# Other places for loads and roundings in a hybrid encoder block: attention's ends, the passage to the mixer, odd blocks' buffers

## The chip, the cores and the metric

The kernel runs on one core of one Trainium2 chip. The metric is the device time of one execution in microseconds (us), as the median of three runs. The engines are TensorE (PE, matmuls; PEld is its weight load), VectorE (DVE), ScalarE (ACT), GpSimd (POOL) and SyncE (SP), which here issues every DMA.

## The reference

One layer of an encoder block on 1024 tokens of width 1024 with 16 learned meta tokens in front, in float32:

```
xn = rmsnorm(h)
q, k, v, xr, gr, gates = split(xn @ w_in)
attn = softmax(rope(norm(q)) rope(norm(k))^T / sqrt(128)) v     # 8 query heads, 2 kv heads of 128, no mask
rnn  = (forward RG-LRU + backward RG-LRU)(conv(xr)) * gelu(gr)
h    = h + (sigmoid(g_attn) * attn + sigmoid(g_rnn) * rnn) @ w_out
h    = h + (silu(n @ w_gate) * (n @ w_up)) @ w_ffn_out          # n = rmsnorm(h), inner width 2816
```

## The kernel before

**Split operands.** A float32 operand is split into a rounded part (hi) and the remainder (lo), and a product of two such operands is three matmuls (hi hi, hi lo, lo hi). `split` (L95 to L97) does it: ACT writes hi (L96), then DVE, or POOL where the caller asks for it, writes lo as source minus hi (L97). So each operand that TensorE reads has a load by SP into a raw buffer, a rounding on ACT and a remainder on DVE or POOL. The pool of raw buffers has three; fifteen larger buffers are called pages.

**Attention** works in tiles (h, i): head h, 128 queries i of 8, all 1040 keys. `emit_scores` multiplies nine matmuls into one of two sets of score banks (S), DVE takes the maximum (L668), ACT the exponential and its sum (L671), which frees the banks, DVE scales the sum and takes its reciprocal (L673, L674). ACT then writes two copies in 16 bit (L677 and the small L678), DVE the residuals (L680, two per tile), and SP issues a transposing DMA. A weighted sum over values (`emit_pv`, 25 matmuls into a bank pv) follows for each pair of tiles, some tiles later; DVE multiplies it with the gate (L696), POOL adds the recurrent part (L697), and the result goes out to memory as the mix.

Between the tiles TensorE gets steps of six matmuls. In heads 0 to 5 they are the gate projection of the next head (`ga_steps`, bank gap, L719 to L721), whose result ACT takes out as a sigmoid (L626). In heads 6 and 7 rests of the gate steps come first and then pieces of the output projection (`out_steps`, bank oph, L763 to L765), which need M (the stored mix, loaded again and split) and wo (blocks of w_out); DVE adds their result to the residual h (L768). The table `ahead` says at which tile each M, wo and x is loaded and split. The gate of head 0 (ga, both halves of the tokens) is projected as a whole before attention begins.

**Passage to the mixer.** The last output tiles (t = 4 to 7) alternate with the second norm. For each token tile DVE makes sums of the transposed rows, which enter the mixer's products as T1 to T4 and B. For t = 4 to 7 POOL adds the hi and lo parts of the lower tokens first (`wholes`), and `norm2_upper` uses the sums.

**Mixer.** The first FFN matrix is done in 22 blocks of 128 columns by a scheme with seven products instead of eight (A11B11, A12B21, S3T3, S2T2, S1T1, A22T4, S4B22), each twelve matmuls. The S operands are sums of quarters of the weight block (`prep`, L966 to L980), made from two raw loads. A11 and A12 of the first three blocks are prepared early (`prep_early`). POOL sums the results of pairs of blocks and the rows of w_ffn_out for the second matrix (`act_sums`, `wout_sums` L1065 to L1068) after every block or pair.

**Order.** The program is written tile by tile. A planner then sets a fixed row of instructions for each engine, by its own estimate of when inputs are there; a row need not follow the program's text, and each engine works its row in order.

## Time and profile before

| | us |
|---|---|
| median of three runs | 1514.45 |
| lowest, highest | 1508.05, 1516.13 |
| the profiled execution | 1514.26 |
| its span | 1512.5 |
| busy: PE, DVE, ACT, POOL | 1477.2, 1090.7, 743.9, 256.9 |

The profiled execution is one run; its span lies between its first and last instruction, and 1.8 us of its time lie outside. Busy time is the time in which an engine executes at least one instruction. The granted clock of PE, 0.993 in the mean, is told as a share of full speed.

### The profile page before, as it was taken

To read this page: it belongs to the slowest core of one execution; us is meant where nothing else is said; L and a number is where in the kernel's file an instruction comes from. 1 tells how busy PE (TensorE), PEld (TensorE's weight loads), DVE (VectorE), ACT (ScalarE), POOL (GpSimd) and SP (SyncE) were. 2 spreads that over 40 slices of the span, in tenths; PEclk is the share of its full clock that TensorE was granted. 3 is DMA by queue.
4 is the path that set the end of the run, shared out by engine and by line. 5 is a ranking of instruction groups with operands and counts; after the bars stand their busy time and mean duration, and the time that the engine had idled before them with its cause. 6 is when DMAs were issued, how large, how long until landed. Compare 5 with 4: busy or idle time off the path is not lost. (4 is left out here: it accounts for less than half of the span.)

```text
span 1512.5 us, 20066 instructions
## 1 busy us (share of the span) xinstructions
PE 1477.2 (98%) x7323; PEld 1240.3 (82%) x7323; DVE 1090.7 (72%) x1695; ACT 743.9 (49%) x1242; POOL 256.9 (17%) x195
## 2 busy tenths in 40 slices
PE   7999999999999899999999999999999999999998
PEld 5888888888888788888778877888888888888887
DVE  6877676666666878777755697888888877557562
ACT  5544477766676676767642452333333332454330
POOL 0000000000000533324320203433333333200000
PEclk9999999999999999999999999999999999999999
DMA  7123311222211789889995216555444444798641
GB/s 245 57 70 98 91 31 61 63 63 63 63 56 57 168 192 198 197 194 235 201 198 174 83 44 194 169 166 165 159 162 155 160 160 153 272 369 286 214 146 58
DMA packets 302275, 222.62 MB, mean 147 GB/s; under 512 B 150776, under 2 KB 244432, under 8 KB 302176
## 3 DMA queue, kind: packets, MB, share of 16 engines
q1 hardware_dynamic: 302176, 221.34, 50.0%
q8 instruction: 57, 0.93, 0.3%
q14 instruction: 42, 0.34, 0.1%
HBM read 133.21 MB, written 52.43 MB: 123 GB/s over the span
## 5 line engine op out<-in xcount | busy, mean ns | idle before, releaser
L96 ACT ACTIVATE pw<-pr 128x1024 fp32r<-128x1024 f32 x77 | 81.1, 1061 | 106.5 <-PE po L1181 63.5
L96 ACT ACTIVATE wS<-s 128x512 fp32r<-128x512 f32 x88 | 53.2, 628 | 151.6 <-DVE s L966 56.8
L1179 PE MATMUL po<-pw 128*128 128x512 f32 x308 | 119.8, 389 | 0.0
L1180 PE MATMUL po<-pw 128*128 128x512 f32 x308 | 119.8, 389 | 0.0
L1181 PE MATMUL po<-pw 128*128 128x512 f32 x308 | 119.8, 389 | 0.0
L97 DVE TENSOR_TENSOR pw<-pr,pw 128x1024 fp32r<-128x1024 f32 x77 | 91.6, 1222 | 37.4 <-ACT pw L96 31.9
L680 DVE SCALAR_TENSOR_TENSOR PP<-p,pr,PP 128x1024 f16<-128x1024 f32 (+1 forms) x128 | 103.1, 864 | 11.8 <-ACT PP L677 11.6
L671 ACT ACTIVATE p<-S,nm 128x1044 f32<-128x1044 f32 x64 | 72.2, 1128 | 52.9 <-DVE nm L668 50.0
L694 PE MATMUL pv<-PT,vt 128*128 128x256 f16 x800 | 94.7, 276 | 2.0 <-DMA PT<-PP 2.0
L97 DVE TENSOR_TENSOR wA<-raw,wA 128x512 fp32r<-128x512 f32 x66 | 72.7, 1125 | 23.6 <-ACT wA L96 23.6
L694 PEld LDWEIGHTS <-vt 128*128 128x128 f16 x800 | 76.5, 99 | 15.6 <-DMA PT<-PP 2.2
L668 DVE TENSOR_REDUCE nm<-S 128x1 f32<-128x1044 f32 x64 | 78.3, 1237 | 6.5 <-PE S L104 6.0
L677 ACT ACTIVATE PP<-p,pr 128x1040 f16<-128x1040 f32 x64 | 73.9, 1154 | 0.0
L102 PE MATMUL S<-kT,qh 128*128 128x348 f32 (+1 forms) x192 | 63.4, 330 | 7.1 <-ACT p L671 7.1
L1181 PEld LDWEIGHTS po<-pw 128*128 128x128 f32 x308 | 57.8, 188 | 12.1
L1179 PEld LDWEIGHTS po<-pw 128*128 128x128 f32 x308 | 57.8, 188 | 12.1
L1180 PEld LDWEIGHTS po<-pw 128*128 128x128 f32 x308 | 57.8, 188 | 11.8
L103 PE MATMUL S<-kT,qh 128*128 128x348 f32 (+1 forms) x192 | 62.7, 327 | 0.0
L104 PE MATMUL S<-kT,qh 128*128 128x348 f32 (+1 forms) x192 | 62.5, 325 | 0.0
L103 PE MATMUL xr<-xn,wblk 128*128 128x264 f32 (+1 forms) x192 | 61.4, 320 | 0.0
L104 PE MATMUL xr<-xn,wblk 128*128 128x264 f32 (+1 forms) x192 | 61.4, 320 | 0.0
L102 PE MATMUL xr<-xn,wblk 128*128 128x264 f32 (+1 forms) x192 | 61.4, 320 | 0.0
(305 smaller groups left out, 4330.4 us busy)
## 6 DMA issues: line engine op xcount, KB each, us to landing
raw<-in_w_ffn_in_dram SPq DMA_DIRECT2D x47, 512.0 KB, 4.7
raw<-in_w_in_dram SPq DMA_DIRECT2D x44, 512.0 KB, 4.1
pr<-act_d SPq DMA_DIRECT2D x77, 256.0 KB, 5.1
...
```

What stands on the lines that cost most here:

```text
L96: S.activation(out=hi, in_=src, func=AF.Copy)
L97: (eng or V).tensor_tensor(out=lo, in0=src, in1=f32(hi), op=ALU.subtract)
L102: PE.matmul(out=ps, lhsT=lh, rhs=rh, start=(k == 0), stop=False)
L103: PE.matmul(out=ps, lhsT=lh, rhs=rl, start=False, stop=False)
L104: PE.matmul(out=ps, lhsT=ll, rhs=rh, start=False, stop=(k == n - 1))
L668: V.tensor_reduce(out=nm, in_=s[:, :, 0:KC], axis=AX.XY, op=ALU.max, negate=True)
L677: S.activation(out=pair[:, 0:NK], in_=pf, func=AF.Copy, scale=r)
L680: V.scalar_tensor_tensor(out=pair[:, o:o + e - a], in0=pf[:, a:e], scalar=r, in1=pair[:, a:e], op0=ALU.mult, op1=ALU.subtract)
L694: PE.matmul(out=ps, lhsT=vt[:, j, hl, vs], rhs=pt[:, m], start=(n == 0), stop=(n == len(terms) - 1))
L1179: PE.matmul(out=banks[t], lhsT=lh, rhs=w[:, 0, 1], start=j == 0, stop=False)
L1180: PE.matmul(out=banks[t], lhsT=lh, rhs=w[:, 1, 1], start=False, stop=False)
L1181: PE.matmul(out=banks[t], lhsT=ll, rhs=w[:, 0, 1], start=False, stop=j == NFP - 1)
```

## The change

- The gate of head 0 is projected for the first half of the tokens only before attention; the second half becomes four steps ahead of the others, and head 0's first five tiles get 3, 3, 2, 2, 2 steps (before 2, 2, 2, 1, 1). A bank is requested once more at the start of its pool, so that the later banks fall on other places.
- In heads 0 to 5 the loads of the next queries and gate weights are separated from their splits, which stand one or two tiles later.
- In heads 6 and 7 every M and wo has its load at one entry of the table and its split at a later one. The remainders are DVE's instead of POOL's, and ACT's rounding stands behind the copies of a tile (`issue_after`). The residual x of the first four token tiles is no longer loaded into h: the first output half is copied there, and x is loaded into a raw buffer and added later by DVE.
- S3, S2 and their splits of block 0 come at t = 4, together with A11 and A12. POOL's sums for t = 7 are gone; DVE subtracts the two parts one by one.
- Blocks with odd number load into a page (wraw) instead of raw buffers. S4's sum is written over S2's. `wout_sums` runs after blocks 4, 5, 6, 8, 9, 10, 12, 14, 16, 18 and 20.

How the rows move: ACT in head 7, around the exponentials (L671 before, L684 after) of tiles (7,4) and (7,5); the copies are PP, and wo is the rounding of a w_out block. Before:

```order
L677 ACTIVATE PP_4463<-p,pr 128x1040
L678 ACTIVATE PP_4463<-p,pr 128x16
L96 ACTIVATE wo<-raw 128x2x512 x2
L671 ACTIVATE p,den<-S_4460,nm 128x1044
L671 ACTIVATE p,den<-S_4461,nm 128x1044
L677 ACTIVATE PP_4464<-p,pr 128x1040
L678 ACTIVATE PP_4464<-p,pr 128x16
L677 ACTIVATE PP_4465<-p,pr 128x1040
L678 ACTIVATE PP_4465<-p,pr 128x16
```

After, from the copies of the pair before:

```order
L690 ACTIVATE PP_4437<-p,pr 128x1040
L691 ACTIVATE PP_4437<-p,pr 128x16
L684 ACTIVATE p,den<-S_4434,nm 128x1044
L684 ACTIVATE p,den<-S_4435,nm 128x1044
L690 ACTIVATE PP_4438<-p,pr 128x1040
L691 ACTIVATE PP_4438<-p,pr 128x16
L98 ACTIVATE wo<-raw 128x2x512
L690 ACTIVATE PP_4439<-p,pr 128x1040
L691 ACTIVATE PP_4439<-p,pr 128x16
L98 ACTIVATE wo<-raw 128x2x512
L684 ACTIVATE p,den<-S_4434,nm 128x1044
L684 ACTIVATE p,den<-S_4435,nm 128x1044
```

Two roundings stood ahead of the exponentials. Now a pair has one between the copies of its two tiles and one behind them, and the next pair's exponentials follow.

DVE in the passage, after the remainder of T3 of t = 7 (T and B are operands of the products, s sums of weights, c and whole sums of rows, act A12B an addition that waits for the product A12B of block 2). Before:

```order
L97 TENSOR_TENSOR T_8034<-c_8220,T_8033 128x4x128
L911 TENSOR_TENSOR c_8218<-c_8218,whole 128x512
L995 TENSOR_TENSOR act<-act,A12B_8246 128x512
L914 TENSOR_TENSOR whole<-whole,c_8218 128x512
L97 TENSOR_TENSOR T_8040<-c_8218,T_8039 128x4x128
L966 TENSOR_TENSOR s_8265<-raw 128x512
L970 TENSOR_TENSOR s_8270<-raw 128x512
L97 TENSOR_TENSOR T_8282<-whole,T_8281 128x4x128
L97 TENSOR_TENSOR wS_8267<-s_8265,wS_8267 128x512
L972 TENSOR_TENSOR s_8272<-s_8270,raw 128x512
L97 TENSOR_TENSOR T_8278<-whole,T_8277 128x4x128
L97 TENSOR_TENSOR T_8282<-whole,T_8281 128x4x128
```

After:

```order
L99 TENSOR_TENSOR T_8058<-c_8245,T_8057 128x4x128
L955 TENSOR_TENSOR c_8250<-hT,B_7782 128x512
L1051 TENSOR_TENSOR act<-act,A12B_8274 128x512
L956 TENSOR_TENSOR c_8250<-c_8250,B_7783 128x512
L99 TENSOR_TENSOR T_8231<-whole,T_8230 128x4x128
L957 TENSOR_TENSOR c_8244<-c_8244,c_8250 128x512
L99 TENSOR_TENSOR T_8226<-whole,T_8225 128x4x128
L963 TENSOR_TENSOR whole<-whole,c_8183 128x512
L99 TENSOR_TENSOR T_8064<-c_8244,T_8063 128x4x128
L99 TENSOR_TENSOR T_8226<-c_8250,T_8225 128x4x128
L99 TENSOR_TENSOR T_8231<-whole,T_8230 128x4x128
L965 TENSOR_TENSOR c_8251<-B_7786,c_8244 128x512
```

S3's sum (L966) and its remainder (wS) are no longer here. T2's remainder, fifth row before, is the ninth row now (T_8064), behind the two subtractions that stand in for POOL's sum (L955, L956) and work on other tiles.

SP from the store of residual rows h on, to the loads of the mixer's weights. Before:

```order
L947 DMA raw<-in_w_ffn_in_dram 128x8x128
L864 DMA h_d_7549<-h 128x1024
L864 DMA h_d_7550<-h 128x1024
L947 DMA raw<-in_w_ffn_in_dram 128x8x128 x2
L1061 DMA raw<-in_w_ffn_out_dram 128x1024 x2
L1044 DMA act_d_7727<-act 128x512
L947 DMA raw<-in_w_ffn_in_dram 128x8x128
L1044 DMA wot_d_7738<-bs 128x512
L947 DMA raw<-in_w_ffn_in_dram 128x8x128
```

After:

```order
L903 DMA h_d_7542<-h 128x1024
L903 DMA h_d_7543<-h 128x1024
L1001 DMA raw<-in_w_ffn_in_dram 128x8x128 x2
L903 DMA h_d_7544<-h 128x1024
L903 DMA h_d_7545<-h 128x1024
L1001 DMA raw<-in_w_ffn_in_dram 128x8x128 x2
L903 DMA h_d_7546<-h 128x1024
L1001 DMA raw<-in_w_ffn_in_dram 128x8x128
L903 DMA h_d_7547<-h 128x1024
L1001 DMA wraw<-in_w_ffn_in_dram 128x8x128 x2
L1001 DMA raw<-in_w_ffn_in_dram 128x8x128
L1001 DMA wraw<-in_w_ffn_in_dram 128x8x128 x2
```

The two loads of w_ffn_out (L1061) stood between the two loads of block 2; now the loads of block 2 stand ahead of the store of h's last rows, and odd blocks have their own loads (wraw).

The diff:

```diff
@@ line 92 @@
         return ap.bitcast(F32)
-    def split(src, hi, lo, eng=None):
-        S.activation(out=hi, in_=src, func=AF.Copy)
+    def split(src, hi, lo, eng=None, behind=None):
+        with tc.issue_after(behind.ins) if behind else nullcontext():
+            S.activation(out=hi, in_=src, func=AF.Copy)
         (eng or V).tensor_tensor(out=lo, in0=src, in1=f32(hi), op=ALU.subtract)
@@ line 177 @@
         return ps0.tile([128, 512], F32, tag=tag, bufs=bufs, name=name)
-    def load_block(col, eng=None):
+    bank0("gate")
+    def load_block(col, eng=None, later=None):
         raw = raw_tile([128, 8, 128])
...
         w = page([128, 2, 8, 128], F32R, "wblk")
-        split(raw, w[:, 0], w[:, 1], eng)
+        if later is None:
+            split(raw, w[:, 0], w[:, 1], eng)
+        else:
+            later.append(lambda: split(raw, w[:, 0], w[:, 1], eng))
         return w
@@ line 629 @@
     w_ga = next_block()
-    for ps, o, n in project("ga", w, REAL):
+    for ps, o, n in project("ga", w, REAL[:1]):
         gate(ga0[:, 0, o:o + n], ps)
@@ line 650 @@
     n_tile = [0]
+    copies = [None]
     PT = {}
@@ line 675 @@
         S.activation(out=pair[:, 0:NK], in_=pf, func=AF.Copy, scale=r)
-        S.activation(out=pair[:, T + 64:T + 64 + NM], in_=pf[:, T:NK], func=AF.Copy, scale=r)
+        copies[0] = S.activation(out=pair[:, T + 64:T + 64 + NM], in_=pf[:, T:NK], func=AF.Copy, scale=r)
         for a, e, o in ((0, T, KLO), (T, NK, T + 32)):
@@ line 708 @@
         return g
-    def ga_steps(w, gar):
-        for c in range(2):
+    def ga_steps(w, gar, chunks=range(2)):
+        for c in chunks:
             ps = fill_bank("gap")
@@ line 725 @@
     M = [[[None, None], [None, None]], [[None, None], [None, None]]]
-    def load_mix(kh, c, eng=None):
-        for hl in range(2):
-            M[hl][kh][c] = page([128, 4, 512], F32R, f"M{hl}{kh}{c}")
-        for k in range(0, 4, 2):
-            n = 1 if kh and not c and k else 2
-            raw = raw_tile([128, 2, 512])[:, 0:n]
-            SP.dma_start(out=raw, in_=mix_d[kh][k:k + n, :, 512 * c:512 * c + 512].rearrange("h d t -> d h t"))
-            split(raw, M[0][kh][c][:, k:k + n], M[1][kh][c][:, k:k + n], eng)
+    def load_mix(kh, c, k, behind=False):
+        if k == 0:
+            for hl in range(2):
+                M[hl][kh][c] = page([128, 4, 512], F32R, f"M{hl}{kh}{c}")
+        n = 1 if kh and not c and k else 2
+        raw = raw_tile([128, 2, 512])[:, 0:n]
+        SP.dma_start(out=raw, in_=mix_d[kh][k:k + n, :, 512 * c:512 * c + 512].rearrange("h d t -> d h t"))
+        yield
+        split(raw, M[0][kh][c][:, k:k + n], M[1][kh][c][:, k:k + n], behind=copies[0] if behind else None)
+        yield
     wo = {}
...
         wo[j, n] = page([128, 2, 2, 512], F32R, "wo")
-        split(raw, wo[j, n][:, :, 0], wo[j, n][:, :, 1], G)
+        yield
+        split(raw, wo[j, n][:, :, 0], wo[j, n][:, :, 1], behind=copies[0])
+        yield
     hres = {}
-    def load_h(c, alloc, js=range(2)):
-        for j in js:
...
@@ line 765 @@
                 hs = hres[t][:, 512 * n:512 * n + 512]
-                V.tensor_tensor(out=hs, in0=hs, in1=ps, op=ALU.add)
+                if kh == 0 and t < 4:
+                    V.tensor_copy(out=hs, in_=ps)
+                else:
+                    V.tensor_tensor(out=hs, in0=hs, in1=ps, op=ALU.add)
             yield
     def out_steps():
+        for j in range(2):
+            p = page([128, 2, D], F32, "h")
+            hres[2 * j], hres[2 * j + 1] = p[:, 0], p[:, 1]
         for n in range(2):
...
     gar = {0: ga0, 1: load_gar(1)}
-    steps = ga_steps(w_ga, gar[1])
+    steps = chain(ga_steps(w, ga0, [1]), ga_steps(w_ga, gar[1]))
+    items = [
+        ("M00a", load_mix, 0, 0, 0, True), ("M00b", load_mix, 0, 0, 2, True), ("w00", load_wout, 0, 0), ("w10", load_wout, 1, 0),
...
+    items = {nm: fn(*a) for nm, fn, *a in items}
     ahead = {
-        (6, 4): [(load_mix, 0, 0, G)],
...
+        (6, 4): ["M00a", "M00b", "w00"],
+        (6, 5): ["w10"],
+        (6, 6): ["w00"],
...
+    later = {}
     for h in range(NH):
...
             emit_scores(h, i, q)
+            for fn in later.pop((h, i), ()):
+                fn()
             if i == 1 and h + 1 < NH:
-                q_n = load_head(h + 1)
+                q_n = load_head(h + 1, later.setdefault((h, 3), []))
+            if i == 2 and h + 2 < NH:
+                w_ga = load_block(COL_GA + 128 * (h + 2), G, later.setdefault((h, 4), []))
             if i == 3 and h + 2 < NH:
-                w_ga = load_block(COL_GA + 128 * (h + 2), G)
                 gar[h + 2] = load_gar(h + 2)
-            for fn, *a in ahead.get((h, i), ()):
-                fn(*a)
+            for nm in ahead.get((h, i), ()):
+                next(items[nm])
             if i == 5 and h + 2 < NH:
@@ line 807 @@
                 pend.append((h, i // 2))
-            for _ in range(2 if h == 0 and i < 3 else 1):
+            for _ in range(1 if h or i > 4 else 2 if i > 1 else 3):
                 next(steps, None)
...
         pass
-    load_mix(0, 1)
+    for k in (0, 2):
+        for _ in load_mix(0, 1, k):
+            pass
     for k in range(4):
...
             pass
-    load_mix(1, 1)
+    for k in (0, 2):
+        for _ in load_mix(1, 1, k):
+            pass
     p2_pool.__exit__(None, None, None)
@@ line 901 @@
         b12, b22 = hn_T(t, y)
-        c1, c4 = bb
-        c22 = tmp("c22")
+        o = slice(128 * (t % 4), 128 * (t % 4) + 128)
+        c22, c3 = tmp("c22"), tmp("c3")
         S.activation(out=c22, in_=b22, func=AF.Copy)
-        c3 = tmp("c3")
         V.tensor_tensor(out=c3, in0=c22, in1=b12, op=ALU.subtract)
         put("T3", t, c3)
-        V.tensor_tensor(out=c1, in0=b12, in1=c1, op=ALU.subtract)
+        if bb:
+            c1, c4 = bb
+            V.tensor_tensor(out=c1, in0=b12, in1=c1, op=ALU.subtract)
+        else:
+            c1, c4 = tmp("c1"), tmp("c4")
+            (h11, l11), (h21, l21) = ([f32(p)[:, :, o] for p in hb(nm)] for nm in ("B11", "B21"))
+            V.tensor_tensor(out=c1, in0=b12, in1=h11, op=ALU.subtract)
+            V.tensor_tensor(out=c1, in0=c1, in1=l11, op=ALU.subtract)
         V.tensor_tensor(out=c22, in0=c22, in1=c1, op=ALU.subtract)
...
         put("B22", t, b22)
-        V.tensor_tensor(out=c4, in0=c4, in1=c22, op=ALU.subtract)
         yield
         put("T1", t, c1)
+        if bb:
+            V.tensor_tensor(out=c4, in0=c4, in1=c22, op=ALU.subtract)
+        else:
+            V.tensor_tensor(out=c4, in0=h21, in1=c22, op=ALU.subtract)
+            V.tensor_tensor(out=c4, in0=c4, in1=l21, op=ALU.add)
         put("T4", t, c4)
@@ line 924 @@
     ys = {}
+    xr = {}
     for t in range(4):
+        xr[t] = raw_tile([128, D])
+        SP.dma_start(out=xr[t], in_=x[128 * t:128 * t + 128])
         out_tile(t, 1, 1)
+        V.tensor_tensor(out=hres[t], in0=hres[t], in1=xr[t], op=ALU.add)
         ys[t] = norm2_rows(t)
@@ line 942 @@
         W[f, nm] = w
-    def load_win(col):
-        r = raw_tile([128, 8, 128])
+    def load_win(col, r=None):
+        r = raw_tile([128, 8, 128]) if r is None else r.rearrange("p (k c) -> p k c", k=8)
         SP.dma_start(out=r, in_=w_ffn_in[:, col:col + 128].rearrange("(k p) c -> p k c", p=128))
...
         return r[:, 0:512], r[:, 512:1024]
-    def prep_early(f):
-        for nm, a in zip(("A11", "A12"), load_win(128 * f)):
+    def prep_early(f, raw=None):
+        for nm, a in zip(("A11", "A12"), raw or load_win(128 * f)):
             wsplit(f, nm, a)
     def prep(f):
-        a11, a12 = load_win(128 * f)
-        a21, a22 = load_win(DFF + 128 * f)
+        r = page([128, 2, D], F32, "wraw") if f % 2 else None
+        a11, a12 = load_win(128 * f, r[:, 0] if f % 2 else None)
+        if f == 0:
+            prep_early(0, (a11, a12))
+            yield
+        a21, a22 = load_win(DFF + 128 * f, r[:, 1] if f % 2 else None)
         if f >= N_EARLY:
@@ line 966 @@
         yield
-        s1 = t2("s1")
+        s1, s2 = t2("s1"), t2("s2")
         V.tensor_tensor(out=s1, in0=a21, in1=a22, op=ALU.add)
-        s2 = t2("s2")
         V.tensor_tensor(out=s2, in0=s1, in1=a11, op=ALU.subtract)
         wsplit(f, "S2", s2)
+        V.tensor_tensor(out=s2, in0=a12, in1=s2, op=ALU.subtract)
         yield
...
         yield
-        s4 = t2("s4")
-        V.tensor_tensor(out=s4, in0=a12, in1=s2, op=ALU.subtract)
-        wsplit(f, "S4", s4)
+        wsplit(f, "S4", s2)
         yield
@@ line 1086 @@
     def up(t):
-        upper[t] = norm2_upper(t, ys.pop(t), ww.pop(t))
+        upper[t] = norm2_upper(t, ys.pop(t), ww.pop(t, None))
         next(upper[t])
...
         ys[t] = norm2_rows(t)
-        if t < 6:
-            prep_early(t - 4)
+        if t == 4:
+            step_prep(0, 3)
         else:
-            up(t - 2)
-            if t == 6:
-                ww[7] = wholes(7)
+            if t > 5:
+                up(t - 2)
+            if t < 7:
+                prep_early(t - 4)
     def run(g):
...
     run(early(0))
-    prep_early(2)
     up(6)
     run(early(1))
+    run(upper[4])
     up(7)
     run(early(2))
-    step_prep(0, 2)
-    for t in range(4, 8):
+    for t in range(5, 8):
         run(upper[t])
     step_prep(0, 5)
+    wout_at = {f: j for j, f in enumerate((4, 5, 6, 8, 9, 10, 12, 14, 16, 18, 20))}
     for f in range(NF):
@@ line 1123 @@
             act_sums(f // 2)
-        else:
-            wout_sums(f // 2)
+        if f in wout_at:
+            wout_sums(wout_at[f])
     flush_stores()
```

## Rows read from the trace of the kernel before

**Rows 1.** The page's busy time of each engine.

```profile
PE 1477.2 (98%) x7323; PEld 1240.3 (82%) x7323; DVE 1090.7 (72%) x1695; ACT 743.9 (49%) x1242; POOL 256.9 (17%) x195
```

**Rows 2.** Windows; columns: stretch, length, each engine's busy time, granted clock, DMA share, GB/s.

```profile
480.00:526.00 46.00, 41.86 (x207) 35.31 (x206) 34.10 (x43) 34.96 (x47) 20.06 (x13) 0.96 0.53 130
700.00:780.00 80.00, 70.93 (x433) 61.73 (x432) 57.67 (x95) 51.50 (x80) 33.42 (x22) 0.94 0.98 217
880.00:926.00 46.00, 38.60 (x152) 29.95 (x152) 36.53 (x58) 14.45 (x26) 5.07 (x4) 0.93 0.32 98
926.00:1506.00 580.00, 580.00 (x2561) 480.25 (x2560) 417.12 (x530) 195.19 (x274) 127.67 (x84) 1.00 0.55 187
```

**Rows 3.** Timeline of PE: start, us, instruction, [idle before, what ended it].

```profile
496.21 0.38 PE L662 MATMUL S<-mask,ones 1*128 1x4 f32 x2 [2.27 <-ACT gar L626]
...
709.59 0.50 PE L719 MATMUL gap<-xn,wblk 128*128 128x512 f32 x1 [1.87 <-ACT gar L626]
...
750.61 4.57 PE L694 MATMUL pv<-PT,vt 128*128 128x256 f16 x25 [1.95 <-DMA PT<-PP]
...
768.43 0.65 PE L102 MATMUL S<-kT,qh 128*128 128x348 f32 x1 [3.49 <-ACT p L671]
...
887.54 0.50 PE L989 MATMUL S3T<-T,wS 128*128 128x512 f32 x1 [3.25 <-ACT wS L96]
...
920.76 0.50 PE L989 MATMUL S3T<-T,wS 128*128 128x512 f32 x1 [3.26 <-ACT wS L96]
```

**Rows 4.** Timeline of ACT and POOL at the start of attention.

```profile
489.38 1.04 ACT L96 ACTIVATE qh<-raw 128x1024 fp32r<-128x1024 f32 x1
...
490.51 2.48 POOL L97 TENSOR_TENSOR qh<-raw,qh 128x1024 fp32r<-128x1024 f32 x1 [62.58 <-ACT qh L96]
...
495.07 1.09 ACT L626 ACTIVATE gar<-ga 128x512 f32<-128x512 f32 x2
```

**Rows 5.** Timeline of DVE and ACT at the start of head 6.

```profile
701.12 5.46 DVE L680 SCALAR_TENSOR_TENSOR PP<-p,pr,PP 128x1024 f16<-128x1024 f32 x4 [0.38 <-ACT PP L677]
...
707.83 1.13 ACT L671 ACTIVATE p<-S,nm 128x1044 f32<-128x1044 f32 x1 [2.87 <-DVE nm L668]
...
711.73 3.03 DVE L680 SCALAR_TENSOR_TENSOR PP<-p,pr,PP 128x1024 f16<-128x1024 f32 x4 [0.36 <-ACT PP L677]
```

**Rows 6.** Timeline of ACT in head 7.

```profile
766.21 1.06 ACT L96 ACTIVATE wo<-raw 128x1024 fp32r<-128x1024 f32 x1 [4.23 <-DMA raw<-in_w_out_dram]
```

**Rows 7.** The page's groups: busy us, mean ns of one, idle before.

```profile
L96 ACT ACTIVATE pw<-pr 128x1024 fp32r<-128x1024 f32 x77 | 81.1, 1061 | 106.5 <-PE po L1181 63.5
...
L97 DVE TENSOR_TENSOR pw<-pr,pw 128x1024 fp32r<-128x1024 f32 x77 | 91.6, 1222 | 37.4 <-ACT pw L96 31.9
...
L671 ACT ACTIVATE p<-S,nm 128x1044 f32<-128x1044 f32 x64 | 72.2, 1128 | 52.9 <-DVE nm L668 50.0
...
L668 DVE TENSOR_REDUCE nm<-S 128x1 f32<-128x1044 f32 x64 | 78.3, 1237 | 6.5 <-PE S L104 6.0
...
L677 ACT ACTIVATE PP<-p,pr 128x1040 f16<-128x1040 f32 x64 | 73.9, 1154 | 0.0
```

**Rows 8.** Timeline of PE behind tile (6,5).

```profile
725.24 2.90 PE L694 MATMUL pv<-PT,vt 128*128 128x256 f16 x25
...
733.91 0.48 PE L763 MATMUL oph<-wo,M 128*128 128x512 f32 x1
```

**Rows 9.** Timeline of POOL and DVE: an addition, residual operations without one.

```profile
711.46 0.73 POOL L697 TENSOR_TENSOR gar<-gar 128x256 f32<-128x256 f32 x1 [1.12 <-DVE gar L696]
...
778.89 2.77 DVE L680 SCALAR_TENSOR_TENSOR PP<-p,pr,PP 128x1024 f16<-128x1024 f32 x4 [0.70 <-ACT PP L677]
```

**Rows 10.** Timeline of DVE and ACT before the mixer's S3 product.

```profile
884.33 0.69 DVE L995 TENSOR_TENSOR act<-act,A12B 128x512 f32<-128x512 f32 x1 [0.26 <-PE A12B L991]
...
886.86 0.63 ACT L96 ACTIVATE wS<-s 128x512 fp32r<-128x512 f32 x1 [0.57 <-DVE s L966]
```

**Rows 11.** Timeline of DVE before block 2's S3 product.

```profile
919.26 0.69 DVE L966 TENSOR_TENSOR s<-raw 128x512 f32<-128x512 f32 x1 [6.45 <-DMA raw<-in_w_ffn_in_dram]
```

More of the change, by code (lines that the diff above doesn't have):

```diff
@@ L1 @@
 import math
-from contextlib import ExitStack
+from itertools import chain
+from contextlib import ExitStack, nullcontext
 import concourse.bass as bass
@@ L596, in scans, with load_head @@
         SP.dma_start(out=rm_d[b], in_=hf)
-    def load_head(h):
+    def load_head(h, later=None):
         raw = raw_tile([128, T])
@@ L601, in load_head @@
         q = page([128, 2, T], F32R, "qh")
-        split(raw, q[:, 0], q[:, 1], G)
+        if later is None:
+            split(raw, q[:, 0], q[:, 1], G)
+        else:
+            later.append(lambda: split(raw, q[:, 0], q[:, 1], G if h < NH - 1 else V))
         return q
@@ L743, in load_wout @@
         wo[j, n] = page([128, 2, 2, 512], F32R, "wo")
-        split(raw, wo[j, n][:, :, 0], wo[j, n][:, :, 1], G)
+        yield
+        split(raw, wo[j, n][:, :, 0], wo[j, n][:, :, 1], behind=copies[0])
+        yield
     hres = {}
-    def load_h(c, alloc, js=range(2)):
-        for j in js:
-            p = alloc([128, 2, D], F32, "h")
-            for i in range(2):
-                t = 4 * c + 2 * j + i
-                hres[t] = p[:, i]
-                SP.dma_start(out=hres[t], in_=x[128 * t:128 * t + 128])
     def out_half(t, n, kh, ps):
@@ L777, in tile_hybrid_encoder_block @@
     gar = {0: ga0, 1: load_gar(1)}
[L778 to L789 removed]
+    steps = chain(ga_steps(w, ga0, [1]), ga_steps(w_ga, gar[1]))
+    items = [
+        ("M00a", load_mix, 0, 0, 0, True), ("M00b", load_mix, 0, 0, 2, True), ("w00", load_wout, 0, 0), ("w10", load_wout, 1, 0),
+        ("w01", load_wout, 0, 1), ("w11", load_wout, 1, 1), ("M10a", load_mix, 1, 0, 0, True), ("M10b", load_mix, 1, 0, 2, True),
+        ("w20", load_wout, 2, 0), ("w30", load_wout, 3, 0), ("w21", load_wout, 2, 1), ("w31", load_wout, 3, 1),
+    ]
+    items = {nm: fn(*a) for nm, fn, *a in items}
+    ahead = {
+        (6, 2): ["M00a", "M00b"],
+        (6, 4): ["M00a", "M00b", "w00"],
+        (6, 5): ["w10"],
+        (6, 6): ["w00"],
+        (6, 7): ["w10"],
+        (7, 0): ["w01"],
+        (7, 1): ["w11"],
+        (7, 2): ["w01"],
+        (7, 3): ["w11"],
+        (7, 4): ["M10a", "M10b"],
+        (7, 5): ["w20"],
+        (7, 6): ["M10a", "M10b", "w30"],
+        (7, 7): ["w20", "w21", "w30", "w31", "w21", "w31"],
     }
+    later = {}
     for h in range(NH):
```

9 lines of the change are left out of this document (1 added, 8 removed).

## The prediction

> **What bounds the kernel now.** I read the page's busy times first: TensorE (PE) is busy 1477.2 of the span's 1512.5 us, VectorE (DVE) 72%, ScalarE (ACT) 49%, GpSimd (POOL) 17% [rows 1]. The change issues the same TensorE instructions in another order, so it can give back only what TensorE loses: its idle time, and stretches at half clock. Where these lie is read from windows. From 926 to 1506 us TensorE is busy for all 580.00 us at a granted clock of 1.00, so nothing is to be had in the mixer behind its first blocks. Three stretches lose: 480 to 526 us idles 4.14 us, 700 to 780 us 9.07 us, 880 to 926 us 7.40 us, 20.6 us together [rows 2]. The remaining 14.7 us of idle time lie at the kernel's first and last microseconds, which the edits don't touch. The same rows show clocks of 0.96, 0.94 and 0.93. Time at 1.2 instead of 2.4 GHz costs half of itself, so the loss is (1 - clock) times the stretch: 1.8, 4.8 and 3.2 us. All that could come back is therefore 6.0 + 13.9 + 10.6 = 30.5 us. TensorE's own rows then name each wait with what ended it [rows 3]. One product of twelve matmuls takes 12 x 580.00 / 2561 = 2.72 us [rows 2].
>
> **Start of attention.** Before, 48 matmuls of head 0's gate (ga) run ahead of the first score tile, and TensorE then waits 2.27 us for ACT's first pass over the gate [rows 3]. After, 24 run ahead and 24 become steps between tiles. The gate's first half then ends at 496.21 - 2.27 - 24 x 0.2265 = 488.5 us. The first score tile meets an operand that is not there: head 0's queries are rounded by ACT until 489.38 + 1.04 = 490.42 and their remainder by POOL until 492.99 [rows 4]. So it waits 1.9 us, then 2.3 us at its third matmul. Behind it stands a gate step, whose bank is free only when ACT's sigmoid pass is done, 495.6 us [rows 4], where score tile 0 ends about 494.1: 1.5 us more. That is 5.7 us of idle time, and I add 1.7 us for one piece at half clock, a third of the 4.8 us that three such pieces cost in head 6 and 7 [rows 2]. 7.4 instead of 6.0 us: **+1.4**. Bounds: -2 (the waits overlap and later ones go, the clock holds) and +5 (a later score tile waits as well, with another clock piece).
>
> **Heads 0 to 5.** Loads come a tile or two earlier and some roundings stand elsewhere. TensorE waits nowhere from 526 to 700 us, so I count 0; if a rounding came late it would show as a wait of a score tile, 1 to 2 us, and that is in the range.
>
> **Heads 6 and 7.** Three things cost the 13.9 us here. (1) At 709.59 TensorE waited 1.87 us for a gate copy of ACT, which stood behind an exponential that waited 2.87 us for DVE's maximum; the maximum came late because four residual operations took 5.46 us instead of 3.03 us [rows 5], beside a POOL rounding. After, the copy stands ahead of the exponential: gone, with its clock piece. (2) At 768.43 it waited 3.49 us for an exponential behind a w_out rounding, which had waited 4.23 us for its load [rows 3, 6]. After, that rounding stands behind the tile's copies and its load is issued a tile earlier: gone. (3) At 750.61 it waited 1.95 us for a transposing DMA.
>
> What is late next is DVE. It takes over eight w_out and four M remainders, 11 x 1.22 + 0.69 = 14.1 us [rows 7, 10], and they lie ahead of maxima. I walked the new rows of ACT and DVE tile by tile. The critical spot is tiles (6,4) and (6,5), with two M roundings between their copies. From the moment tile (6,5)'s scores are ready: maximum 1.24, exponential 1.13, first copy 1.15, two ACT roundings 2.12, second copy 1.15, two residual operations 1.5, maximum 1.24 and exponential 1.13 of tile (6,6), with some 1.4 of short copies, sums and issue between them (an estimate): 12.1 us until a score bank is free. TensorE has 733.91 - 725.24 = 8.7 us of work for that time, a weighted sum, two score tiles and a weighted sum [rows 7, 8], so 3.4 us of idle time and one clock piece of 1.7. The same walk at (7,2) and (7,3), with one rounding of ACT and two of DVE in the chain but two more output steps on TensorE, leaves 1.1 us before tile (7,6). The products that use the third w_out block wait for its remainder, which DVE reaches behind two of M: 2.5 us, and a clock piece in one case of two, 0.9. Together 3.4 + 1.7 + 1.1 + 2.5 + 0.9 = 9.6 us against 13.9: **-4**. Bounds: -13.9 (all waits go) and +9 (worked out with the rivals).
>
> Here the remaining POOL work matters. Four residual operations take 2.77 us with POOL idle and 3.03 us beside one POOL addition of 0.73 us [rows 5, 9], 0.26 us each. Seven such additions remain in the two heads, 1.8 us if all hit the chain; I leave that in the range. The Trainium skill ("SBUF — State Buffer", Who interferes with whom) says that a VectorE instruction with two SBUF inputs contends with a GpSimd one that reads SBUF, and that the loser blocks for a whole instruction. By that rule the moved remainders are no longer disturbed by POOL's, and each addition could cost its whole 0.73 us, 5.1 us instead of 1.8. The 0.26 us measured lie below it.
>
> **Passage to the mixer.** At 887.54 TensorE waited 3.25 us for the rounded S3 of block 0, which ACT had only after DVE's sum [rows 3, 10]. DVE worked back to back there. After, S3 and S2 of block 0 are made some 40 us earlier, so this wait goes. But the upper-half tile of t=7 now gets two more DVE operations, since POOL no longer sums its halves, and S2's product needs that tile's T2. From the add of A12B at 884.33 [rows 10], which waits for the same product as before, the new DVE row has six operations until T2's remainder; at 0.60 us apart it ends at 884.33 + 7 x 0.60 + 0.1 = 888.6. S3's product ends at 884.14 + 2.72 = 886.9, so TensorE now waits 1.6 us at S2, with a clock piece in one case of two, 0.9. The stretch from 880 to 926 us idles 7.40 us, 3.25 and 3.26 of it in the two long waits of this part and the next and the rest in short repeats behind them, so each part had half of 7.40 + 3.2: 5.3 us. After: 2.5. **-2.8**. Bounds: -5.3 (DVE is ahead) and 0 (the wait only moves).
>
> **Block 2.** At 920.76 TensorE waited 3.26 us, because DVE's S3 waited 6.45 us for a raw load [rows 3, 11] that queued on a buffer held by POOL's sums for w_ffn_out. After, odd blocks load into pages, the two loads of block 2 are issued before the passage (ahead of t=6's store), and the first such sum waits until block 4. All of its half goes: **-5.3**. Bounds: -5.5 and -2 (a new wait of half the size). POOL's later sums and the page loads run where TensorE had no idle time; I cost them at 0, hidden by loads issued a block ahead.
>
> **Sum.** +1.4 - 4.0 - 2.8 - 5.3 = -10.7. The profiled execution took 1514.26 us (span 1512.5 and 1.8 around it), close to the median of 1514.45. 1514.3 - 10.7 = 1503.6, which I round to **1503 us**.
>
> **Rivals.**
> - Every wait but the start's goes: 1514.3 + 1.4 - 13.9 - 5.3 - 5.3 = 1491. For it: in the 580 us behind, DVE at 72% keeps TensorE full. Against it: the walk finds 14.1 us more DVE work in a chain that already ended waits. Chance 0.13.
> - DVE swallows the gain in heads 6 and 7 (0 instead of -4, by a longer chain or POOL's additions): 1507.6; or the start costs its upper bound: 1507. Either leaves the time within 0.5%. Chance 0.21.
> - Slower: DVE becomes the bound of heads 6 and 7. If all 14.1 us of remainders lie in the chain from maximum to maximum, and only the stretched residuals come back (5.46 - 3.03 = 2.4, and I take as much once more in head 7: 4.9), these heads lose 9.2 us; the same backlog leaves the passage at 0. 1514.3 + 1.4 + 9.2 - 5.3 = 1519.6. It decides from a loss of some 12 us here, so that block 2 no longer pays for it. Against it: between (7,0) and (7,4) no pair has more than two remainders and TensorE has output steps to fill. Chance 0.06.
> - The edit at the start not doing what it says is already in the sum: the steps are there, but TensorE waits ahead of them.
>
> **How the numbers follow.** The forecast has 0.60, with 1499 to 1507 as its own range. 0.5% (7.6 us) is about what a measurement of this kernel tells from no change. Faster by more: the first rival and nearly all of the forecast, 0.71. Same: the second rival with the forecast's edge, 0.23. Slower: 0.06. The range of 1492 to 1512 us leaves out half of the first rival, the third, and the worst of the second.
>
> **What would show it.** In the new profile: about 5.5 us of TensorE waits around 488 to 496 us, first on the queries' rounding; no wait on the gate copy at head 6's start; a wait of 3 to 4 us ahead of a score tile about (7,0) ended by ACT's exponential behind DVE; S3's product without a wait and S2's with 1 to 2 us on DVE's T; no wait at block 2. If 700 to 780 us loses over 14 us, or TensorE waits anywhere from 930 us on, the prediction is wrong.

## The result and the profile after

The changed kernel takes 1501.55 us (median of six runs, 1499.36 to 1503.84); six runs of the kernel before have a median of 1512.31 us. The ratio is 0.9923, 95% interval 0.9911 to 0.9936: 0.77% faster. The profiled execution took 1499.36 us with a span of 1497.6 us, 14.9 us below that of before, while the ratio stands for 11.6 us of 1512.3; so a single pair of traces is good to some 3 us.

The page of the kernel after, busy time of each engine:

```profile
PE 1471.2 (98%) x7323; PEld 1236.3 (83%) x7323; DVE 1112.7 (74%) x1714; ACT 743.5 (50%) x1242; POOL 222.3 (15%) x180
```

Against [rows 1] DVE has 22.0 us more and POOL 34.6 us less. Windows of the kernel after, columns as in [rows 2]:

```profile
480.00:526.00 46.00, 42.28 (x206) 35.38 (x205) 33.02 (x39) 32.78 (x44) 16.33 (x12) 0.93 0.50 129
700.00:780.00 80.00, 76.29 (x468) 66.66 (x467) 66.68 (x109) 51.55 (x79) 7.53 (x11) 0.96 0.82 186
780.00:865.00 85.00, 82.39 (x413) 68.17 (x412) 60.22 (x104) 31.21 (x54) 9.45 (x8) 1.00 0.53 173
865.00:926.00 61.00, 59.70 (x270) 48.63 (x268) 57.82 (x97) 28.88 (x51) 5.46 (x4) 1.00 0.35 108
926.00:1492.00 566.00, 566.00 (x2499) 468.68 (x2498) 411.95 (x507) 186.41 (x262) 132.30 (x84) 1.00 0.56 188
```

From 700 to 780 us TensorE idles 3.71 us where it idled 9.07 [rows 2]. A wait of 2.61 us is new behind 780 us, and the passage with block 2 idles 1.30 us. The waits that remain, from the timeline of PE after (what ended the wait stands in brackets):

```profile
489.50 0.51 PE L104 MATMUL S<-kT,qh 128*128 128x348 f32 x1 [1.67 <-ACT qh L98]
...
492.03 0.66 PE L106 MATMUL S<-kT,qh 128*128 128x348 f32 x1 [1.72 <-POOL qh L99]
...
494.74 0.80 PE L732 MATMUL gap<-xn,wblk 128*128 128x512 f32 x1 [0.33 <-ACT gar L637]
...
732.74 0.66 PE L104 MATMUL S<-kT,qh 128*128 128x348 f32 x1 [3.17 <-ACT p L684]
...
775.93 0.50 PE L778 MATMUL S<-wo,M 128*128 128x512 f32 x1 [0.55 <-DVE wo L99]
...
791.66 0.50 PE L777 MATMUL S<-wo,M 128*128 128x512 f32 x1 [2.61 <-DVE h L785]
...
882.56 0.50 PE L1045 MATMUL S2T<-T,wS 128*128 128x512 f32 x1 [0.86 <-ACT T L98]
...
883.71 0.50 PE L1046 MATMUL S2T<-T,wS 128*128 128x512 f32 x1 [0.41 <-DVE T L99]
```

Of the six waits of [rows 3] five are gone and the one at the start is replaced by its first three rows here. [rows 3] leaves out a wait of 1.87 us at 514.54, gone too, and this one, ahead of tile (7,0) in the kernel before:

```profile
735.99 0.43 PE L102 MATMUL S<-kT,qh 128*128 128x348 f32 x1 [1.60 <-ACT p L671]
```

The 3.17 us are ahead of the same tile, so this wait grew. Which part gave how much is read from a ledger: the start of one and the same TensorE instruction in both traces, after minus before.

| instructions up to | after - before, us | by this part |
|---|---|---|
| the last instructions ahead of attention (480) | -0.96 | -0.96, at 17 us already, in unchanged code |
| heads 0 to 5 (600, the same at 700) | -0.49 | start of attention +0.47 |
| output products in head 7 (788) | -8.36 | -7.9 |
| the second norm (850) | -5.65 | +2.7, the wait at 791.66; heads 6 and 7 together -5.2 |
| S3's product of block 1 (905) | -9.42 | passage -3.8 |
| S4's product of block 1 (916) | -9.47 | 0 |
| A22's product of block 2 (933), the same at 1390 | -15.34 | block 2 -5.9 |

### The profile page after: what moved, and what is told of

The parts are those of the page before. It is cut to its first block, busy times and chain, and to the rows that moved or that the text cites. A ratio compares the mean times of both kernels' runs of the same rounds, so it can differ in the third digit from the quotient of the medians.

```text
span 1497.6 us, 20061 instructions
## 1 busy us (share of the span) xinstructions
PE 1471.2 (98%) x7323; PEld 1236.3 (83%) x7323; DVE 1112.7 (74%) x1714; ACT 743.5 (50%) x1242; POOL 222.3 (15%) x180
## 5 line engine op out<-in xcount | busy, mean ns | idle before, releaser
L684 ACT ACTIVATE p<-S,nm 128x1044 f32<-128x1044 f32 x64 | 72.3, 1130 | 69.1 <-DVE nm L681 55.8
L99 DVE TENSOR_TENSOR wS<-s,wS 128x512 fp32r<-128x512 f32 x88 | 69.3, 805 | 0.0
L1106 POOL TENSOR_TENSOR as<-act 128x512 f32<-128x512 f32 x11 | 17.8, 1615 | 315.9 <-DVE act L1094 290.5
L105 PE MATMUL xr<-xn,wblk 128*128 128x264 f32 (+1 forms) x192 | 61.4, 320 | 0.0
L106 PE MATMUL xr<-xn,wblk 128*128 128x264 f32 (+1 forms) x192 | 61.4, 320 | 0.0
```

The source lines that it names most:

```text
L99: (eng or V).tensor_tensor(out=lo, in0=src, in1=f32(hi), op=ALU.subtract)
L105: PE.matmul(out=ps, lhsT=lh, rhs=rl, start=False, stop=False)
L106: PE.matmul(out=ps, lhsT=ll, rhs=rh, start=False, stop=(k == n - 1))
```

## Experiments

Ratios are to the kernel before, measured on the same chip beside it; the interval is 95%. The edits are to the changed kernel where nothing else is said. The chips differ from one experiment to another (the kernel before has medians of 1512.31 to 1514.58 us), so ratios are what compares. In 6 to 8 the interval overlaps with the changed kernel's; there the waits and the ledger tell more than the time.

**1. The start undone (u_start): 1500.81 us, 0.9912 (0.9893 to 0.9931).**

```diff
-    for ps, o, n in project("ga", w, REAL[:1]):
+    for ps, o, n in project("ga", w, REAL):
-    steps = chain(ga_steps(w, ga0, [1]), ga_steps(w_ga, gar[1]))
+    steps = ga_steps(w_ga, gar[1])
-            for _ in range(1 if h or i > 4 else 2 if i > 1 else 3):
+            for _ in range(2 if h == 0 and i < 3 else 1):
```

> The changed kernel with the start of attention as before: all 48 matmuls of head 0's gate ahead of the first score tile, no extra steps. Theory (the edit at the start is worth little or nothing, the profile's lead there falls by 0.5 us): TensorE waits about 2.3 us ahead of the first score tile for the gate's pass and perhaps 1.9 us with a half-clock piece at tile 4; the time is within 3 us of the changed kernel's (1499 to 1504). Rival (refilling the start is what gains): the time is 5 us or more above the changed kernel's.

The waits on the queries vanish, and one score tile waits instead, with a stretch of 3.41 us at half clock behind it. Timeline of PE:

```profile
513.93 0.43 PE L104 MATMUL S<-kT,qh 128*128 128x348 f32 x1 [3.56 <-ACT p L684]
```

Its ledger over this part is -0.15 us, against +0.47 in the changed kernel. The 2.3 us for the gate's pass, which I expected ahead of the first score tile, did not come; the extra bank request at the start of the pool was kept here, and no run undoes it. The order of the gate's steps exchanges waits of one kind for waits of another and brings nothing.

**2. Remainders of heads 6 and 7 back on POOL, places kept (u_pool): 1508.24 us, 0.9965 (0.9949 to 0.9982).**

```diff
-  split(raw, M[0]..., M[1]..., behind=copies[0] if behind else None)
+  split(raw, M[0]..., M[1]..., G if behind else None, behind=copies[0] if behind else None)
-  split(raw, wo[j, n][:, :, 0], wo[j, n][:, :, 1], behind=copies[0])
+  split(raw, wo[j, n][:, :, 0], wo[j, n][:, :, 1], G, behind=copies[0])
```

> The changed kernel with the remainders of M and w_out in heads 6 and 7 back on POOL, all places kept. Theory (the gain in these heads is the earlier loads and the roundings behind the copies; DVE's extra work costs a part of it, POOL's remainders stretch the residual operations to about 5 us where they meet): the wait of 3.2 us ahead of tile (7,0) shrinks or moves, 700 to 780 us loses 5 to 9 us (now 7), the time is within 4 us of the changed kernel's. Rival (moving the remainders to DVE is what gains): residual operations of 4.9 to 5.5 us come back at several tiles, 700 to 780 us loses 11 us or more, and the time is 5 us or more above the changed kernel's.

By the ratios 6.4 us of the 11.6 are lost, so the rival held in the time: with these places the remainders on DVE are where the gain is, not its price. (700 to 780 us loses 9.5 us and not the rival's 11; 1.53 and 3.71 us of waits follow behind 780.) The same stretch of DVE in the two kernels shows why. u_pool first, DVE and then POOL:

```profile
726.12 3.80 DVE L693 SCALAR_TENSOR_TENSOR PP<-p,pr,PP 128x1024 f16<-128x1024 f32 x2 [0.36 <-ACT PP L690]
729.85 2.38 DVE L681 TENSOR_REDUCE nm<-S 128x1 f32<-128x1044 f32 x2
...
736.36 3.52 DVE L693 SCALAR_TENSOR_TENSOR PP<-p,pr,PP 128x1024 f16<-128x1024 f32 x2
```

```profile
727.32 4.88 POOL L99 TENSOR_TENSOR M<-raw,M 128x1024 fp32r<-128x1024 f32 x2 [0.73 <-ACT M L98]
...
737.19 4.99 POOL L99 TENSOR_TENSOR wo<-raw,wo 128x1024 fp32r<-128x1024 f32 x2 [2.42 <-ACT wo L98]
```

And the changed kernel, DVE:

```profile
724.92 1.69 DVE L693 SCALAR_TENSOR_TENSOR PP<-p,pr,PP 128x1024 f16<-128x1024 f32 x2 [0.36 <-ACT PP L690]
726.53 2.35 DVE L99 TENSOR_TENSOR M<-raw,M 128x1024 fp32r<-128x1024 f32 x2
728.80 1.42 DVE L693 SCALAR_TENSOR_TENSOR PP<-p,pr,PP 128x1024 f16<-128x1024 f32 x2
730.14 2.38 DVE L681 TENSOR_REDUCE nm<-S 128x1 f32<-128x1044 f32 x2
```

Two residual operations take 3.80 and 3.52 us while POOL subtracts, and 1.42 us alone (1.69 beside a short addition of POOL). Nearly all of it falls on the second, small one, which comes up when POOL's subtraction has begun and ends with it; u_pool, DVE:

```profile
727.59 2.33 DVE L693 SCALAR_TENSOR_TENSOR PP<-p,pr,PP 128x16 f16<-128x16 f32 x1
```

The first one, already running, takes 1.55 us in both kernels. By form, u_pool and then the changed kernel:

```profile
L693 DVE SCALAR_TENSOR_TENSOR PP<-p,pr,PP 128x16 f16<-128x16 f32 x18 | 15.1, 840 | 0.0
```

```profile
L693 DVE SCALAR_TENSOR_TENSOR PP<-p,pr,PP 128x16 f16<-128x16 f32 x18 | 4.1, 226 | 0.0
```

Grouped over 700 to 780 us (count, then busy time and mean ns), u_pool and then the changed kernel:

```profile
L693 DVE SCALAR_TENSOR_TENSOR PP<-p,pr,PP 128x1024 f16<-128x1024 f32 (+1 forms) x36 | 39.8, 1153 | 3.3 <-ACT PP L690 3.2
```

```profile
L693 DVE SCALAR_TENSOR_TENSOR PP<-p,pr,PP 128x1024 f16<-128x1024 f32 (+1 forms) x36 | 26.2, 779 | 1.5 <-ACT PP L690 1.5
L99 DVE TENSOR_TENSOR wo<-raw,wo 128x1024 fp32r<-128x1024 f32 x6 | 7.3, 1218 | 1.2 <-ACT wo L98 1.2
L99 DVE TENSOR_TENSOR M<-raw,M 128x1024 fp32r<-128x1024 f32 (+1 forms) x4 | 4.2, 1080 | 0.0
```

The residuals shrink by 13.6 us, 11.0 of it in the small ones, and the ten remainders cost DVE 11.5 us: for these groups DVE is busy 37.7 us instead of 39.8, with POOL's work in it. The Trainium skill ("SBUF — State Buffer", Who interferes with whom) says that a VectorE instruction with two SBUF inputs contends with a GpSimd one that reads SBUF, and that the engine that comes second blocks while the first holds the shared ports for its whole instruction; these rows agree (0.22 us alone, 2.33 beside a subtraction of 2.58 us).

**3. The engine alone (b_dve, edits to the kernel before): 1512.11 us, 0.9994 (0.9977 to 1.0011).**

```diff
-        split(raw, wo[j, n][:, :, 0], wo[j, n][:, :, 1], G)
+        split(raw, wo[j, n][:, :, 0], wo[j, n][:, :, 1])
...
-        (6, 4): [(load_mix, 0, 0, G)],
+        (6, 4): [(load_mix, 0, 0)],
...
-        (7, 4): [(load_mix, 1, 0, G)],
+        (7, 4): [(load_mix, 1, 0)],
```

> The kernel before with one edit: the remainders of M and w_out in heads 6 and 7 on DVE instead of POOL, loads and roundings where they were. Theory (a remainder on POOL beside the residual operations stretches them by about its own length, so DVE loses nothing by taking it over; the loads' late places cost the rest): residual operations fall from 0.94 to about 0.78 us in the mean, the wait at 709.59 goes, the waits on exponentials behind late loads at 735 and 768 stay; 2 to 5 us faster than before. Rival (DVE is the bound and pays 1.2 us for each remainder): waits in 700 to 780 us grow, the time is 2 us or more above before.

The stretch goes here too (a residual operation takes 781 ns in the mean from 700 to 780 us, 944 before), and yet nothing is gained: weighted sums now wait for their transposing DMAs. Timeline of PE:

```profile
730.14 1.05 PE L694 MATMUL pv<-PT,vt 128*128 128x256 f16 x8 [2.41 <-DMA PT<-PP]
...
769.41 1.01 PE L694 MATMUL pv<-PT,vt 128*128 128x256 f16 x4 [4.99 <-DMA PT<-PP]
```

A likely reason is in the row of ACT, where w_out roundings still wait for their loads ahead of the copies and exponentials; b_dve:

```profile
755.25 1.06 ACT L96 ACTIVATE wo<-raw 128x1024 fp32r<-128x1024 f32 x1 [1.42 <-DMA raw<-in_w_out_dram]
...
760.37 1.06 ACT L96 ACTIVATE wo<-raw 128x1024 fp32r<-128x1024 f32 x1 [1.70 <-DMA raw<-in_w_out_dram]
```

So the engine alone gives 0 in the time, and neither the theory's time nor the rival's came; its ledger over heads 6 and 7 is -0.8 us. The places of loads and roundings without the engine make these heads slower: in u_pool's ledger they cost 3.3 us, against -5.2 in the changed kernel. Both together make the gain. (The later addition of the residual x is in u_pool too and was not undone by itself.)

**4. Odd blocks in raw buffers again (u_raw): 1502.17 us, 0.9921 (0.9903 to 0.9938).**

```diff
-        r = page([128, 2, D], F32, "wraw") if f % 2 else None
+        r = page([128, 2, D], F32, "wraw") if False else None
...
```

> The changed kernel with odd blocks loading into the three raw buffers again, the sums for w_ffn_out still late. Theory (block 2's wait went because POOL's sums no longer hold a raw buffer at blocks 0 and 2): no wait of over 1 us at block 2, and TensorE stays full later; time within 2 us of the changed kernel's. Rival (the pages are what frees the loads): a wait of 2 to 4 us at S3's product of block 1 or 2 comes back, time 3 to 6 us above.

**5. POOL's sums for w_ffn_out after every even block again, pages kept (u_wout): 1502.39 us, 0.9915 (0.9901 to 0.993).**

```diff
-        if f in wout_at:
-            wout_sums(wout_at[f])
+        else:
+            wout_sums(f // 2)
```

> The changed kernel with POOL's sums for w_ffn_out after every even block again (0, 2, 4, ...), odd blocks still in pages. Theory (the sums held raw buffers that block 2 needed): a wait of 2 us or more at S3's product of block 2 comes back, time 3 to 6 us above the changed kernel's. Rival (with odd blocks in pages the raw buffers suffice anyway): no wait over 1 us at block 2, time within 2 us.

**6. Both (u_both): 1504.06 us, 0.9943 (0.9924 to 0.9962).** The edit is that of 4 and 5.

> The changed kernel with both parts of the block-2 edit undone: odd blocks load into the three raw buffers and POOL's sums for w_ffn_out run after every even block. Theory (either part alone is enough, only both together make the raw buffers short): a wait of 2.5 to 4 us at S3's product of block 2 comes back, the lead there is 4 to 6 us smaller than the changed kernel's, time 3 to 6 us above it. Rival (the loads' places on SP, ahead of the store of h, are what cured it): no wait over 1 us at block 2.

In 4 and in 5 TensorE is busy for all 30 us from 905 to 935, and the ledger over block 2 gains 5.9 us in each, as in the changed kernel. Only with both undone does the wait come back, smaller than before. Timelines of PE and DVE in u_both:

```profile
911.33 0.50 PE L1045 MATMUL S3T<-T,wS 128*128 128x512 f32 x1 [1.19 <-ACT wS L98]
...
912.53 0.50 PE L1047 MATMUL S3T<-T,wS 128*128 128x512 f32 x1 [0.47 <-DVE wS L99]
```

```profile
909.86 0.69 DVE L1024 TENSOR_TENSOR s<-raw 128x512 f32<-128x512 f32 x1 [5.20 <-DMA raw<-in_w_ffn_in_dram]
```

Its ledger gains 2.0 us there. Either the pages or the later sums free the raw buffer in time; my theory in 5, that the sums had to be late, fell. What shortened the wait from 3.26 us [rows 3] to 1.19 us without both was not tried by itself; what is left of the change there is above all that the block's loads stand further ahead on SP.

**7. S3 and S2 of block 0 not early (u_early): 1504.04 us, 0.9934 (0.9913 to 0.9954).**

```diff
-            step_prep(0, 3)
+            step_prep(0, 1)
...
     run(early(2))
+    step_prep(0, 2)
```

> The changed kernel with S3 and S2 of block 0 made behind the last upper tile as before; DVE still sums for t = 7. Theory (S3's early place is what took the wait of 3.25 us away): TensorE waits 3 us or more at S3's product of block 0 with a half-clock piece, and the lead there is 4 to 6 us smaller than the changed kernel's; time 4 to 6 us above it. Rival (the wait went because DVE's row had less ahead for another reason): the wait stays under 1.5 us, the time within 2 us.

S3's wait is back; timeline of PE:

```profile
881.37 0.50 PE L1045 MATMUL S3T<-T,wS 128*128 128x512 f32 x1 [2.39 <-ACT wS L98]
```

The wait is shorter than the 3 us that I expected, and half clock follows it (3.41 us). The passage gains 0.7 us in its ledger, 3.8 in the changed kernel's.

**8. POOL's sums for t = 7 back, S3 early (n_wholes): 1504.93 us, 0.9937 (0.9922 to 0.9952).**

```diff
                 up(t - 2)
+                if t == 6:
+                    ww[7] = wholes(7)
```

> The changed kernel with POOL's two sums for t = 7 back. Theory (the two short waits at S2's product, 0.86 and 0.41 us, come from DVE's extra operations for t = 7): both go, lead in the passage 1 to 1.3 us larger, no other change. Rival (POOL's sums disturb DVE's operations or T2 is late anyway): waits of 0.8 us or more stay at S2, time unchanged within 1 us.

I expected a gain from fewer DVE operations; the theory fell. S3's product waits again, now for its other operand T:

```profile
885.88 0.49 PE L1045 MATMUL S3T<-T,wS 128*128 128x512 f32 x1 [3.06 <-ACT T L98]
```

The passage gains 0.4 us in the ledger. So each edit is needed here as well. Why T is late isn't settled: the edit also moved DVE's row, in which the difference for t = 7's T3 (L946) now starts at 884.15 behind an addition for A12B (L1051), where it stood ahead of that addition in the changed kernel. Whether POOL's sums or this order costs the wait was not tried.

**9. Head 0's query remainder on DVE (n_qdve): 1502.24 us, 0.9918 (0.9902 to 0.9935).**

```diff
-            split(raw, q[:, 0], q[:, 1], G)
+            split(raw, q[:, 0], q[:, 1], V)
```

> The changed kernel with head 0's query remainder on DVE, which is idle then, instead of POOL. Theory (the second wait of the first score tile, 1.72 us, is POOL's 2.48 us remainder): that wait falls to about 0.5 us, but the gate step behind the tile waits for ACT's pass until 494.7 in any case, so TensorE idles about as long in all and the time is within 1.5 us of the changed kernel's. Rival (the remainder bounds the start): the total idle time from 487 to 497 us falls by 1 us or more and one half-clock piece goes, time 2 to 3 us below.

The wait at the third matmul shrinks from 1.72 to 0.86 us, and the gate step behind it waits that much longer for ACT:

```profile
491.02 0.66 PE L106 MATMUL S<-kT,qh 128*128 128x348 f32 x1 [0.86 <-DVE qh L99]
...
494.81 0.80 PE L732 MATMUL gap<-xn,wblk 128*128 128x512 f32 x1 [1.40 <-ACT gar L637]
```

3.93 us of waits instead of 3.72: ACT's sigmoid, done at 494.76, sets the end of this stretch, with two table loads of 1.28 us and two passes of the recurrent part ahead of it.

**10. The new wait (n_mixpool): 1497.75 us, 0.9891 (0.9876 to 0.9906).** In the changed kernel the wait at 791.66 ends on DVE; the rounding on ACT and DVE's rows there:

```profile
788.38 1.06 ACT L98 ACTIVATE M<-raw 128x1024 fp32r<-128x1024 f32 x1 [0.91 <-DMA raw<-mix_d]
...
789.47 1.54 DVE L99 TENSOR_TENSOR M<-raw,M 128x1024 fp32r<-128x1024 f32 x1 [0.41 <-ACT M L98]
...
790.93 0.68 DVE L785 TENSOR_TENSOR h<-h,S 128x512 f32<-128x512 f32 x1
```

The addition that frees the bank stands behind an M remainder whose rounding waited for its load. The edit gives the remainders of M that are not tied to a tile's copies to POOL:

```diff
-  split(raw, ..., behind=copies[0] if behind else None)
+  split(raw, ..., None if behind else G, behind=copies[0] if behind else None)
```

> The changed kernel with the remainders of M's second token half (the four roundings behind the last tile) on POOL. Theory (the new wait of 2.61 us at 791.66 is DVE held by a remainder that waits for its load, so that the copy that frees a score bank comes late): the wait goes, time 2 to 3 us below the changed kernel's. Rival (the bank is late for another reason, or POOL's slower remainder becomes the wait at the products that read M): a wait of 1.5 us or more stays within 785 to 850 us, no gain.

2.61 us become 0.63 and 1.03:

```profile
788.02 1.03 PE L707 MATMUL pv<-PT,vt 128*128 128x256 f16 x8 [0.63 <-DVE h L783]
...
790.08 0.63 PE L777 MATMUL S<-wo,M 128*128 128x512 f32 x1 [1.03 <-DVE h L785]
```

The wait is 0.95 us shorter in sum. The median lies 3.8 us below the changed kernel's, and the two intervals of the ratio don't overlap. Where the rest lies this profile cannot show: it is of the slowest of the four runs, 1500.05 us, and loses 3.3 us in its ledger here, where the changed kernel's loses 2.7. The record points at the clock: this run has 0.994 in the mean, the other three 0.996 to 0.997, an estimated 3 to 4.5 us less lost to half clock. And in seven of the nine traces that have the long wait (2.49 to 3.71 us) 3.41 or 6.83 us at half clock stand at it or right behind; the changed kernel's own trace, one of its two fastest runs, is one of the two without. With the shorter wait two of three traces (those of 10, 11 and 12) have none. So a shorter wait probably saves such a stretch in most runs; that is argued from these counts, not shown.

**11. The wait ahead of tile (7,0) by place (n_mspread, with the edit of 10): 1497.78 us, 0.9902 (0.9886 to 0.9918).**

```diff
-        (6, 4): ["M00a", "M00b", "w00"],
-        (6, 5): ["w10"],
+        (6, 4): ["M00a", "w00"],
+        (6, 5): ["M00b", "w10"],
```

> The changed kernel with the two M roundings of (6,4) put one on each side of the second tile's copies, and the remainders of M's second token half on POOL. Theory (the 3.17 us wait ahead of tile (7,0) is the chain through both M roundings and both remainders between the residual operations): the wait falls by 1 to 2 us, the wait at 791 to about 1 us; time 1 to 4 us below the changed kernel's. Rival (DVE's total work between the maxima is what counts, not the place): the wait ahead of (7,0) stays at 3 us or more, time within 1.5 us.

The wait stays, 3.16 us against 3.17. DVE now has one remainder behind each tile's residuals, and the maxima (TENSOR_REDUCE) follow as late:

```profile
725.83 1.69 DVE L693 SCALAR_TENSOR_TENSOR PP<-p,pr,PP 128x1024 f16<-128x1024 f32 x2 [0.36 <-ACT PP L690]
727.43 1.21 DVE L99 TENSOR_TENSOR M<-raw,M 128x1024 fp32r<-128x1024 f32 x1
728.57 1.42 DVE L693 SCALAR_TENSOR_TENSOR PP<-p,pr,PP 128x1024 f16<-128x1024 f32 x2
729.91 1.21 DVE L99 TENSOR_TENSOR M<-raw,M 128x1024 fp32r<-128x1024 f32 x1
731.05 2.38 DVE L681 TENSOR_REDUCE nm<-S 128x1 f32<-128x1044 f32 x2
```

**12. One M remainder out of that pair (n_mearly, with the edit of 10): 1497.01 us, 0.9895 (0.9879 to 0.9912).**

```diff
-        (6, 2): ["M00a", "M00b"],
-        (6, 4): ["M00a", "M00b", "w00"],
+        (6, 0): ["M00a", "M00b"],
+        (6, 2): ["M00a"],
+        (6, 4): ["M00b", "w00"],
```

> The changed kernel with the second-half remainders of the mixer's block M back on POOL, as in n_mixpool, and one rounding of M two steps earlier, so that the pair of score tiles ahead of (7,0) has one M remainder fewer on DVE. Theory (what bounds the tile (7,0) is DVE's work between two maxima, wherever in the pair it stands): the wait ahead of (7,0) falls from 3.2 us to about 1 to 2 us, and the time is 1 to 3 us below n_mixpool's 1497.75 us. Rival (the remainder holds up the earlier pair by as much, or its rounding waits for its load there): the wait appears one pair earlier, and the time is within 1.5 us of n_mixpool's.

```profile
734.48 0.42 PE L104 MATMUL S<-kT,qh 128*128 128x348 f32 x1 [1.98 <-ACT p L684]
...
736.68 0.50 PE L777 MATMUL oph<-wo,M 128*128 128x512 f32 x1 [0.51 <-ACT wo L98]
```

Tile (7,0), now at 730.81, no longer waits; its neighbour (7,1), the first row, waits 1.98 us. So the wait moved by a tile and fell by 1.2 us, one remainder, as the theory has it: in a pair DVE's whole work between two maxima counts. The median falls by only 0.74 us and the ratio not at all (0.9895 after 0.9891), as the rival has it: 0.51 us appear at the products behind, 1.11 us at the next weighted sum's transposing DMA and 0.36 us ahead of tile (6,6). These three versions, 1497 to 1498 us, beat both kernels; they can't be told from one another.

## Why the prediction was right, and which step failed

- **Sum.** -10.7 was forecast; the ratio gives -11.6, the one pair of traces -14.9.
- **Start, +1.4 forecast, +0.47 measured.** The first two waits came as worked out (1.67 and 1.72 us for 1.9 and 2.3). The third was 0.33 instead of 1.5, because score tile 0 itself ran at half clock and ended later: its matmuls start 0.29 us apart (492.48 to 493.93), against 0.16 us at full clock. The idle time was 3.72 us instead of 5.7; of the 6.83 us at half clock 2.05 were idle anyway, so they cost some 2.4 us instead of 1.7. That the gate's steps are worth nothing is shown by experiment 1.
- **Heads 6 and 7, -4 forecast, -5.2 measured, by another account.** The walk from tile (6,5) to the exponential ahead of (7,0) was right: 3.4 us worked out, 3.17 measured, ended by ACT's exponential behind DVE. The 1.1 us at (7,6) did not come, and the 2.5 us at the third w_out block were 0.55. The 2.61 us at 791.66 were in no step: I walked the rows only to the last score tiles, and there a late load held up DVE's row. The total came out right by luck: 9.6 us of loss were forecast, and 3.17 + 0.55 + 2.61 and about 3.1 for the 6.83 us at half clock are 9.4, from other terms.
- **The step that failed** is the price of DVE's added work: 14.1 us taken over as a cost, against which the slower rival sets 4.9 us of stretched residuals that come back. The size of the remainders was right (ten of about 1.2 us in the stretch), and 4.9 is near what the kernel before loses (33 residuals at 944 instead of 781 ns, 5.4 us). But in the new places POOL's remainders stretch the residuals by 13.6 us, more than the 11.5 us of DVE's own (experiment 2); so the move is what makes the earlier places pay. I had priced the block per instruction only for POOL's short additions, at 0.26 us; beside a subtraction it is 2.1 us. The sum does not rest on this step, since the walk took the residuals unstretched.
- **Passage, -2.8 forecast, -3.8 measured.** S3's wait went. S2's product waits 0.86 and 0.41 us instead of the 1.6, on the same chain, and no half clock followed. Experiments 7 and 8: each of the two edits without the other brings 0.4 to 0.7 us.
- **Block 2, -5.3 forecast, -5.9 measured.** The buffer was the cause, as argued; the pages and the later sums, which I named side by side, do the same: one suffices (experiments 4 to 6).
- **Heads 0 to 5 at 0:** TensorE is busy for all 174.00 us from 526 to 700 us, as before.
- **Slips in the working:** 888.6 - 886.9 is 1.7 and not 1.6, a third of 4.8 is 1.6 and not 1.7, and 1503.6 rounds to 1504. None matters to the forecast.
